# Low halves of W_in and of three more weight pieces: from VectorE and GpSimd to VectorE alone, in the first phase of a hybrid decoder layer

## The chip, the cores and the metric

The kernel runs on one core of one Trainium2 chip. The metric is device time in microseconds of one execution; lower is better. The time before is the median of three runs, 245.26 us (245.08 to 245.63).

## The reference, cut to what matters

One layer on a sequence of 512 rows and 1024 columns, float32 throughout:

```
shift, scale, gate = SiLU(c) @ W_ada + b_ada
h = RMSNorm(x) * (1 + scale) + shift
z = h @ W_in          # [lru_x | lru_gate | q | k | v | attn_gate], 3072 columns
lru_x -> causal conv(4) -> block-diagonal gates -> linear recurrence -> * SiLU(lru_gate)
q, k, v -> per-head RMS norm of q, k -> block attention (256-row blocks) -> * SiLU(attn_gate)
out = x + gate * (concat(groups) @ W_out)
```

Products must have nearly float32 precision. The kernel gets it by splitting each operand into a high half (rounded to the format that TensorE multiplies fast) and a low half, low = value - high, and by adding three products: high by high, low by high and high by low.

## The kernel before, in words

**Tiling.** The contraction runs over 1024 columns, so over eight slices (k = 0 to 7) of 128. Phase 1 computes the first 896 columns of `z`, transposed: four tiles xl0 to xl3 (the recurrent input) and three tiles gl0 to gl2 (its gate), seven PSUM banks that accumulate over the eight slices. For each slice, TensorE runs 14 matmuls with the high half of h (against the high and low weight) and then 7 with the low half of h (against the high weight): 21 matmuls of 512 columns, in a fixed order.

**What a slice needs.** From memory come a 1 MB piece of W_ada (`st`, in two halves) and a 0.45 MB piece of W_in in two parts, `wa` (512 columns) and `wb` (384). For slices 2 to 7, VectorE makes scale and shift from `st` with two dot products against the broadcast SiLU(c) (L442) and two tiny steps (`gs`, L483 and L484). ScalarE then writes h in float32 (`hf`, L495) and its high half (`h2h` and so on, L503), and VectorE the low half (`h2l`, L267). The weights are split by `split` (L271): the high half is a copy (`wA2h`, `wB2h`, L257, nearly all on ScalarE) and the low half a subtraction (`wA2l`, `wB2l`, L267).

**After phase 1.** VectorE and ScalarE read the seven banks: a convolution for each xl tile (`xc`, one ScalarE step L632 and three VectorE steps L635) and tanh-based SiLU for each gl tile (`gg`, L641 and L642). TensorE goes on with k: four row tiles k0 to k3, first half of the contraction with weight piece 0, second half with piece 1; then q with pieces 2 and 3, v with 8 and 9. k0 goes into bank 3, and k1, k2, k3 into banks 0, 1, 2, which gl0, gl1 and gl2 held: k1 can start when gg0 has been read out. A weight piece is 1 MB (`w_piece`, L554): one DMA into a staging buffer `wp0`, `wp1`, ..., four high halves and four low halves of 512 columns each (`w0_0h`, `w0_0l` to `w0_3l`). There are three staging buffers, shared by `st` and `wp` pieces: a piece's DMA is issued when the last reader of an older piece is done. In the profile numbers are left out of a name in places, so `w_2l` may be the third low half of any piece. Between the halves of k come `pr` (L654), the gates' block-diagonal products, which need xc.

**What sets the order.** A planner (`Plan`, L66 to L218) takes every step with its cost on each engine that may run it and a due time, and builds one list for each engine by a list schedule in estimated time. The lists are then fixed: each engine works through its own strictly in order, waiting on semaphores. Where a step may run on several engines, the planner takes the one that by its estimate finishes first. A subtraction of `split` may go to VectorE or GpSimd, unless `dve_only` is set; it was set for slices 0 and 1. The planner also knows a lock, so that in its estimate VectorE and GpSimd don't work at the same time where both use SBUF:

```
    def locks(o, e):
        return e == "POOL" or (e == "DVE" and o.sbuf)
```

Of the kernel before, what the change touches and what calls it, by code (L numbers as in the profile page):

```python
# [31 lines left out]
RESERVE = 10  # L32
SAME, SWITCH = 0.13, 0.1
EPS_PICK, ALPHA = 0.2, 0.1
NPE = 2
NSTAGE = 3
NC1 = 896
T0, TK, LEAD, NWARM, WSTEP, DIP = 14.5, 5.2, 4.0, 18, 0.35, 0.8
RAW, EPS0, ALPHA0, LATER = 3, 0.35, 1.0, 15.5
# [23 lines left out]
class Plan:  # L63
# [10 lines left out]
    def slot(self, name, dt=F32, n=512):  # L74
        return Buf(name, "slot", dt, n)
# [13 lines left out]
    def op(self, fn, costs, reads=(), writes=(), out_lat=None, dl=None, rel=0.0, window=None, sbuf=None, bulk=False, bias=None, mode="full"):  # L89
        o = Op(len(self.ops), fn, costs, out_lat)  # L90
        o.mode = mode
        o.bulk, o.bias = bulk, self.bias if bias is None else bias
        o.est, o.sbuf, o.free = rel, True, window
        for lst, wr in ((reads, False), (writes, True)):
            for x in lst:
                b, key = x if isinstance(x, tuple) else (x, None)
                if b.prev is not None:
                    o.preds.update(b.prev.ops)
                for k2, (ws, rs) in b.state.items():
                    if key is None or k2 is None or key == k2:  # L100
                        o.preds.update(ws)
                        if wr:
                            o.preds.update(rs)
                if wr:
                    if key is None:
                        b.state = {}
                    b.state[key] = ([o], [])
                else:
                    b.state.setdefault(key, ([], []))[1].append(o)
                if not b.ops or b.ops[-1] is not o:  # L110
                    b.ops.append(o)
                o.bufs.append(b)
                if b.kind == "bank":
                    o.sbuf = False
        if sbuf is not None:
            o.sbuf = sbuf
        o.preds.discard(o)
        for p in o.preds:
            p.succs.append(o)
        o.own = "PE" in costs and dl is None  # L120
        if "PE" in costs:
            o.dl = o.want = self.pe_t
            self.pe_t += costs["PE"]
        if dl is not None:
            o.dl = dl
        self.ops.append(o)
        return o
# [93 lines left out]
def c_act(n, ap=0, ps=False):  # L221
    return (0.052 if ps else 0.095) + n / 1200 + 0.093 * ap
# [15 lines left out]
def hybrid_layer_kernel(ctx: ExitStack, tc, x, small, call, bgate, wbd, wad, w1, wp, out):  # L238
# [8 lines left out]
    def fixed(name, shape, dt=F32):  # L247
        return Buf(name, "fixed", t=cp.tile(shape, dt, name=name))


    def copy(dst, d_ap, src, s_ap, n, psum=False, scale=None, reads=(), bulk=False, bias=None):

        ap = 0 if scale is None else 1

        def fn(e):
            if e is act:
                act.activation(d_ap(), s_ap(), AF.Copy, scale=1.0 if scale is None else scale())  # L257
            elif scale is None:
                dve.tensor_copy(d_ap(), s_ap())
            else:  # L260
                dve.tensor_scalar(d_ap(), s_ap(), scale(), None, op0=MULT)
        return op(fn, {"ACT": c_act(n, ap, psum), "DVE": c_dve(n, ap, psum, not psum)}, [src, *reads], [dst],
                  bulk=bulk, bias=bias)

    def tt(dst, d_ap, a, a_ap, b, b_ap, n, alu, psum=False, dve_only=False, rel=0.0):
        def fn(e):
            e.tensor_tensor(d_ap(), a_ap(), b_ap(), op=alu)  # L267
        costs = {"DVE": c_dve(n)} if psum or dve_only else c_tt(n)
        return op(fn, costs, [a, b], [dst], rel=rel)

    def split(src, s_ap, n, name, bulk=False, dve_only=False, rel=0.0):  # L271

        h, l = slot(name + "h", F32R, n), slot(name + "l", F32R, n)
        copy(h, lambda: h.t[:, :n], src, s_ap, n, bulk=bulk)
        tt(l, lambda: l.t[:, :n], src, s_ap, h, lambda: h.f()[:, :n], n, SUB,
           dve_only=dve_only, rel=rel)
        return h, l


    def dma(fn, mb, writes, extra=0.0, **kw):  # L280
        ndma[0] += 1
        if ndma[0] < 45 and "dl" not in kw:
            kw["dl"] = 0.001 * ndma[0]
        return op(lambda e: fn(), {"DMA": 0.05 + mb * 2.55 + extra}, [], writes, out_lat=2.0, **kw)
# [44 lines left out]
    def mk_gm(e):  # L329
# [4 lines left out]
                                 op1=MULT)  # L334
        dve.tensor_scalar(gm.t[:, NPE:, :], gm.t[:, NPE:, :], 0.5, None, op0=MULT)
    op(mk_gm, {"DVE": 0.6}, [sm], [gm, ga_], sbuf=False)
# [53 lines left out]
    for t in range(NT):  # L390
        w = xw[t // 2]
# [26 lines left out]
    NA, NB = 512, NC1 - 512  # L418
# [9 lines left out]
    hh, hl, ada, W1 = [None] * KT, [None] * KT, {}, {}  # L428

    def load_ada(k):  # L430
# [3 lines left out]
        for q in range(2):  # L434
            dma(lambda q=q: sp.dma_start(st.t[:, q * 1024:(q + 1) * 1024], wad[k, :, q * 1024:(q + 1) * 1024]), 0.5,
                [(st, q)], (DIP, 0.1, 0.1)[k] if k < 3 and q == 0 else 0.0)
        if k >= NPE:
            m = ada[k] = fixed(f"m{k}", [P, 2])
# [24 lines left out]
    def load_w(k):  # L463
        a, b = slot(f"wa{k}"), slot(f"wb{k}", n=NB)
        dma(lambda: sp.dma_start(a.t, w1[k, :, :512]), 0.25, [a])
        dma(lambda: sp.dma_start(b.t[:, :NB], w1[k, :, 512:]), 0.25 * NB / 512, [b])
        W1[k] = (split(a, lambda: a.t, 512, f"wA{k}", dve_only=k < 2, rel=0.0 if k else LATER),
                 split(b, lambda: b.t[:, :NB], NB, f"wB{k}", dve_only=k < 2, rel=0.0 if k else LATER))

    def gs_make(k):  # L470
        if k < NPE:
            acc = ada[k]

            def mm(e):
                for o in (0, 1):
                    pe.matmul(misc.t[:, 2 * k + o:2 * k + o + 1], acc.t[:, o * P:(o + 1) * P], ones.t[:, 0:1], start=True,
                              stop=True)
            op(mm, {"PE": 0.46}, [acc, ones], [(misc, k)], dl=T0 - 1.8 if k == 0 else T_[k] - 7.0)
        src = (misc, k) if k < NPE else ada[k]

        def mk(e):
            m, g = misc.t[:, 2 * k:2 * k + 2] if k < NPE else ada[k].t, gs.t[:, k, :]
            dve.tensor_tensor(g, m, gm.t[:, k, :], op=MULT)  # L483
            dve.tensor_tensor(g, g, ga_.t[:, k, :], op=ADD)  # L484
        op(mk, {"DVE": 0.3}, [src, gm, ga_], [(gs, k)], sbuf=False)
# [30 lines left out]

    load_ada(0)
    load_w(0)
    cb = fixed("cb", [P, D])
    load_ada(1)  # L520
    gs_make(0)
    h_make(0)
    load_w(1)
    for i in range(2):
        c_ = slot(f"c{i}")
        dma(lambda i=i, c_=c_: sp.dma_start(c_.t, call[:, i * 512:(i + 1) * 512]), 0.25, [c_])
        v = lambda i=i: cb.t[:, i * 512:(i + 1) * 512]
        op(lambda e, v=v, c_=c_: act.activation(v(), c_.t, AF.Tanh, scale=0.5), {"ACT": c_act(512, 0)}, [c_], [(cb, i)],
           dl=T_[NPE] - 8.0)
        op(lambda e, v=v, c_=c_: dve.scalar_tensor_tensor(v(), v(), 1.0, c_.t, op0=ADD, op1=MULT),  # L530
# [3 lines left out]
    gs_make(1)  # L534
    h_make(1)
    load_w(2)
    load_ada(3)
    for k in range(KT):
# [15 lines left out]
    def w_piece(i, n=4):  # L554
        st = Buf(f"wp{i}", "stage")
        dma(lambda: sp.dma_start(st.t[:, :n * 512], wp[i, :, :n * 512]), 0.25 * n, [st])
        return [split(st, lambda j=j: st.t[:, j * 512:(j + 1) * 512], 512, f"w{i}_{j}", True) for j in range(n)]

    def gated_w(dh, c, cn):

# [315 lines left out]
    zb = [3, 0, 1, 2]  # L876
    kb_ = [bank(f"k{t}", zb[t]) for t in range(4)]
    z_half(kb_, w_piece(0), True, True, [None, None, None, lambda: (gates(0, (4, 5)), gates(1, (6, 7)))])
    z_half(kb_, w_piece(1), True, False, [None, None, lambda: (gates(2, (4, 5)), gates(3, (6, 7)))])
    for t in range(4):  # L880
        qk_norm(kb_[t], ("k", t))
    qb_ = [bank(f"q{t}", zb[t]) for t in range(4)]
    z_half(qb_, w_piece(2), True, True, [None] + [lambda t=t: qk_tr(("k", t), 4 + t) for t in range(3)])
    lru_sqrt()
    z_half(qb_, w_piece(3), True, False, [lambda: qk_tr(("k", 3), 7)])
# [33 lines left out]
    for i in range(len(items)):  # L919
# [11 lines left out]
        a, hps = items[i]  # L931
# [17 lines left out]
    n = 0  # L949
    for o in pl.schedule():  # L950
        for b in o.bufs:
            if b.t is None:
# [5 lines left out]
                else:  # L958
                    w = b.n if b.kind == "slot" else 2048
# [64 lines left out]
```

## Time and profile before

| | |
|---|---|
| median of three runs | 245.26 us |
| the profiled execution, its own time | 243.45 us |
| its span, first to last instruction | 241.6 us |
| TensorE busy | 230.7 us, 95% |
| VectorE busy | 176.9 us, 73% |
| ScalarE busy | 140.4 us, 58% |
| GpSimd busy | 72.5 us, 30% |
| TensorE clock granted, mean | 0.999 |

All rows in the text come from the one profiled execution. PE is TensorE, DVE VectorE, ACT ScalarE, POOL GpSimd, and SP or SPq is SyncE, whose queue issues every DMA. A row of a timeline has the start in us from the span's beginning, the duration, engine, line of the kernel, operation, what is written and read with its shape, and in brackets the idle time ahead of it with the instruction that ended it. Consecutive instructions of one engine overlap by some tens of ns, so a cost is best read as the distance from one start to the next.

### The profile page before, as it was taken

To read this page: it belongs to the slowest core of one execution; us is meant where nothing else is said; L and a number is where in the kernel's file an instruction comes from. 1 tells how busy PE (TensorE), PEld (TensorE's weight loads), DVE (VectorE), ACT (ScalarE), POOL (GpSimd) and SP (SyncE) were. 2 spreads that over 40 slices of the span, in tenths; PEclk is the share of its full clock that TensorE was granted. 3 is DMA by queue.
4 is the path that set the end of the run, shared out by engine and by line. 5 is a ranking of instruction groups with operands and counts; after the bars stand their busy time and mean duration, and the time that the engine had idled before them with its cause. 6 is when DMAs were issued, how large, how long until landed. Compare 5 with 4: busy or idle time off the path is not lost.

```text
span 241.6 us, 3603 instructions
## 1 busy us (share of the span) xinstructions
PE 230.7 (95%) x1270; PEld 183.3 (76%) x1270; DVE 176.9 (73%) x389; ACT 140.4 (58%) x287; POOL 72.5 (30%) x66
## 2 busy tenths in 40 slices
PE   8899997999599999999999999999999999999994
PEld 8666875787387778888888768777777888788894
DVE  0779999979998578459667488596999996287221
ACT  5856453498528796334034379998999997131000
POOL 3300443207531462449320211329047122000001
PEclk9999999999999999999999999999999999999999
DMA  6999998770670402510470863000006012812221
GB/s 223 351 404 401 399 383 278 255 275 39 226 297 0 174 0 88 195 68 1 152 255 30 343 203 152 1 0 20 27 0 254 9 53 77 260 46 88 90 84 47
DMA packets 11879, 37.77 MB, mean 156 GB/s; under 512 B 1362, under 2 KB 3922, under 8 KB 9812
## 3 DMA queue, kind: packets, MB, share of 16 engines
q1 hardware_dynamic: 11860, 37.53, 42.7%
q8 instruction: 10, 0.16, 0.3%
q14 instruction: 9, 0.07, 0.1%
HBM read 35.43 MB, written 2.10 MB: 155 GB/s over the span
## 4 chain that ended last, share of the span: by engine, by line
PE 65%; DVE 18%; DMA 9%; ACT 5%; issue 2%; SPq 1%; DVEq 0%; ACTq 0%
PE u L842 19%; PE g L866 9%; PE q L616 9%; PE k L616 8%; PE v L616 6%; DVE st L442 5%; PE PT L803 4%; PE pv L820 4%; DMA st<-in_wad_dram 4%; DMA c<-in_call_dram 3%; PE S L765 3%; DVE ga L590 2%; DMA wg<-in_wp_dram 2%; PE pr L654 1%; DVE w_2l L267 1%
## 5 line engine op out<-in xcount | busy, mean ns | idle before, releaser
L778 ACT ACTIVATE P<-P,st 128x512 f32<-128x512 f32 (+3 forms) x32 | 17.6, 556 | 3.6 <-DVE st L775 3.6
L442 DVE SCALAR_TENSOR_TENSOR st<-st,cb 128x1024 f32<-128x1024 f32 x12 | 17.6, 1494 | 0.0
L787 POOL TENSOR_SCALAR P<-P,st 128x384 f32<-128x384 f32 (+3 forms) x13 | 9.0, 698 | 25.6 <-DVE st L781 25.6
L267 DVE TENSOR_TENSOR o<-u,gbc 128x512 f32<-128x512 f32 (+1 forms) x8 | 5.3, 658 | 14.5 <-PE u L842 14.5
L495 ACT ACTIVATE hf<-xs,gs 128x512 f32<-128x512 f32 x8 | 6.5, 814 | 15.8 <-DVE gs L484 15.8
L775 DVE CUSTOM_DVE_ANT_0 P<-S,maskf 128x512 f32<-128x512 f32 (+3 forms) x32 | 14.3, 481 | 0.9 <-PE g L866 0.9
L590 DVE SCALAR_TENSOR_TENSOR ga<-wg,cs,ga 128x512 f32<-128x512 f32 x16 | 12.8, 833 | 2.1 <-DMA wg<-in_wp_dram 2.1
L257 ACT ACTIVATE pt<-PT 128x384 f32<-128x384 f32 (+1 forms) x23 | 11.1, 526 | 3.4 <-PE PT L803 3.2
L267 POOL TENSOR_TENSOR w_1l<-wp,w_1h 128x512 fp32r<-128x512 f32 x4 | 6.4, 1599 | 20.5 <-ACT w_1h L257 13.8
L803 PE MATMUL PT<-ident,P 128*128 128x128 f32 x80 | 11.4, 277 | 0.3 <-ACT P L785 0.3
L803 PEld LDWEIGHTS PT<-ident,P 128*128 128x128 f32 x80 | 9.0, 141 | 3.1 <-issue 1.1
L267 POOL TENSOR_TENSOR o<-xr,o 128x256 f32<-128x256 f32 x1 | 0.7, 738 | 34.6 <-DVE o L267 34.6
L711 POOL TENSOR_TENSOR msk<-msk,nhalf 128x8 f32<-128x8 f32 x4 | 7.0, 1757 | 11.0 <-DVE msk L709 11.0
L820 PE MATMUL pv<-pt,vt 128*64 128x256 f32 (+1 forms) x96 | 10.0, 350 | 0.0
L711 POOL TENSOR_TENSOR msq<-msq,nhalf 128x8 f32<-128x8 f32 x4 | 7.8, 1952 | 6.0 <-DVE msq L709 5.9
L267 DVE TENSOR_TENSOR w_0l<-wp,w_0h 128x512 fp32r<-128x512 f32 x10 | 8.5, 849 | 1.5 <-ACT w_0h L257 1.5
L785 ACT ACTIVATE P<-P,st 128x128 f32<-128x128 f32 (+3 forms) x19 | 9.5, 544 | 0.0
L820 PEld LDWEIGHTS pv<-pt,vt 128*64 128x64 f32 x96 | 6.4, 136 | 4.0 <-issue 1.2
L257 ACT ACTIVATE qTh<-Tq 128x512 fp32r<-128x512 f32 x4 | 2.4, 598 | 11.2 <-PE Tq L723 11.2
L267 POOL TENSOR_TENSOR w_3l<-wp,w_3h 128x512 fp32r<-128x512 f32 x4 | 5.6, 1408 | 9.7 <-ACT w_3h L257 9.7
L635 DVE SCALAR_TENSOR_TENSOR xc<-xl,sm,xc 128x511 f32<-128x511 f32 (+2 forms) x12 | 8.0, 732 | 0.0
L422 PE MATMUL warm<-warm 128*128 128x128 bf16 x72 | 6.7, 277 | 1.0 <-DVE warm L304 1.0
(718 smaller groups left out, 787.6 us busy)
## 6 DMA issues: line engine op xcount, KB each, us to landing
wp<-in_wp_dram SPq DMA_DIRECT2D x12, 1024.0 KB, 4.8
st<-in_wad_dram SPq DMA_DIRECT2D x16, 512.0 KB, 7.5
wg<-in_wp_dram SPq DMA_DIRECT2D x4, 1024.0 KB, 4.8
x<-in_x_dram SPq DMA_DIRECT2D x4, 512.0 KB, 5.5
wa<-in_w_dram SPq DMA_DIRECT2D x8, 256.0 KB, 7.7
xr<-in_x_dram SPq DMA_DIRECT2D x7, 256.0 KB, 2.8
out_dram<-o SPq DMA_DIRECT2D x7, 256.0 KB, 2.0
wb<-in_w_dram SPq DMA_DIRECT2D x8, 192.0 KB, 7.5
```

What stands on the lines that cost most here:

```text
L257: act.activation(d_ap(), s_ap(), AF.Copy, scale=1.0 if scale is None else scale())
L267: e.tensor_tensor(d_ap(), a_ap(), b_ap(), op=alu)
L442: dve.scalar_tensor_tensor(v, v, 1.0, cb.t, op0=MULT, op1=MULT, accum_out=m.t[:, q:q + 1])
L590: dve.scalar_tensor_tensor(gacc[hf].t, w, cs.t[:, d:d + 1], gacc[hf].t, op0=MULT, op1=ADD)
L616: pe.matmul(acc.t, hx[kt].t[:, a * P:(a + 1) * P], wx.t, start=s0, stop=s1)
L711: op(lambda e: pool.tensor_tensor(m.t, m.t, nhalf.t, op=ALU.pow), {"POOL": 1.65}, [nhalf], [m])
L775: op(lambda e: dve.tensor_tensor_reduce(p_.t[:, :n], b.t[:, c0:c0 + n], maskf.t[:, 512 - n:], -1.0, -NEG, op0=ADD, op1=ALU.min, accum_out= ...
L778: op(lambda e: act.activation(p_.t[:, :n], p_.t[:, :n], AF.Exp, bias=st.t[:, 0:1], scale=-1.0, accum_out=st.t[:, 1:2]), {"ACT": c_act(n, 2 ...
L803: pe.transpose(b.t[:, o_:o_ + P], p_.t[:, kb * P:(kb + 1) * P], ident.t)
L820: pe.matmul(b.t[64 * e_:64 * e_ + 64, h0 + o_:h0 + o_ + n], vt[kb].t[:, hd * 64:(hd + 1) * 64], pt[e_, kb // 2].t[:, 256 * (kb % 2):256 * ...
L842: pe.matmul(b.t[:, :cn], y_.t[:, c0:c0 + P], w.t[:, cw:cw + cn], start=kt == 0 and i == 0, stop=kt == KT - 1 and i == 2)
L866: pe.matmul(b.t, wx.t[:, c0:c0 + P], hx[kt].t, start=kt == 0 and p == 0, stop=kt == KT - 1 and p == 2)
```

## The change

A constant `NDV = 3` is added, and `dve_only` is set in three calls of `split`: for both parts of W_in in all eight slices (before: slices 0 and 1), and for the weight pieces 0, 1 and 2. Their subtractions may then run on VectorE only. Nothing else is written differently.

```
+NDV = 3
...
-        W1[k] = (split(a, lambda: a.t, 512, f"wA{k}", dve_only=k < 2, rel=0.0 if k else LATER),
-                 split(b, lambda: b.t[:, :NB], NB, f"wB{k}", dve_only=k < 2, rel=0.0 if k else LATER))
+        W1[k] = (split(a, lambda: a.t, 512, f"wA{k}", dve_only=True, rel=0.0 if k else LATER),
+                 split(b, lambda: b.t[:, :NB], NB, f"wB{k}", dve_only=True, rel=0.0 if k else LATER))
...
-        return [split(st, lambda j=j: st.t[:, j * 512:(j + 1) * 512], 512, f"w{i}_{j}", True) for j in range(n)]
+        return [split(st, lambda j=j: st.t[:, j * 512:(j + 1) * 512], 512, f"w{i}_{j}", True, dve_only=i < NDV) for j in range(n)]
```

The planner then builds other lists. TensorE's list is the same, row for row. GpSimd's loses eleven subtractions and gains one. Its list between the last step for x and the gates, before (the added line makes every line number one larger afterwards):

```order
L267 TENSOR_TENSOR wA2l_59_463<-wa2_47_412,wA2h_53_445 128x512
L267 TENSOR_TENSOR wA3l_69_513<-wa3_54_447,wA3h_63_487 128x512
L267 TENSOR_TENSOR wA4l_81_570<-wa4_65_494,wA4h_74_540 128x512
L267 TENSOR_TENSOR wA5l_92_622<-wa5_73_535,wA5h_78_560 128x512
L267 TENSOR_TENSOR wA6l_103_671<-wa6_82_577,wA6h_88_606 128x512
L267 TENSOR_TENSOR wA7l_115_720<-wa7_90_616,wA7h_98_646 128x512
L267 TENSOR_TENSOR w1_3l_138_801<-wp1_102_665,w1_3h_123_749 128x512
L267 TENSOR_TENSOR w2_0l_142_817<-wp2_113_714,w2_0h_127_765 128x512
L267 TENSOR_TENSOR w2_1l_146_830<-wp2_113_714,w2_1h_129_771 128x512
L267 TENSOR_TENSOR w2_2l_149_843<-wp2_113_714,w2_2h_132_780 128x512
L267 TENSOR_TENSOR w2_3l_150_852<-wp2_113_714,w2_3h_148_836 128x512
L267 TENSOR_TENSOR xcs0l_153_865<-xc0_134_786,xcs0h_151_855 128x512
```

All but the last are gone from GpSimd's list afterwards; it goes from the steps for x straight to xcs0l, and does w8_2l much later, which VectorE did before. The second place is VectorE's list in phase 1, from the end of slice 2's dots on (`gs` is scale and shift, `po` a chain of twelve small steps for the softplus of the recurrence, which ends in `sp4` and `sn4`). Before:

```order
L483 TENSOR_TENSOR gs_93<-m2_95,gm_74 128x2
L484 TENSOR_TENSOR gs_93<-gs_93,gad_75 128x2
L358 TENSOR_SCALAR po_82<-z2_81 128x4
L360 SCALAR_TENSOR_TENSOR po_82<-po_82,z2_81 128x4 x3
L267 TENSOR_TENSOR wB2l_61_480<-wb2_49_419,wB2h_55_451 128x384
L442 SCALAR_TENSOR_TENSOR st3_50_425,m3_96<-st3_50_425,cb_94 128x1024 x2
L267 TENSOR_TENSOR h2l_68_509<-hf2_60_470,h2h_62_482 128x512
L483 TENSOR_TENSOR gs_93<-m3_96,gm_74 128x2
L484 TENSOR_TENSOR gs_93<-gs_93,gad_75 128x2
L360 SCALAR_TENSOR_TENSOR po_82<-po_82,z2_81 128x4 x4
L267 TENSOR_TENSOR wB3l_71_530<-wb3_57_457,wB3h_64_491 128x384
```

VectorE at the same place now:

```order
L484 TENSOR_TENSOR gs_93<-m2_95,gm_74 128x2
L485 TENSOR_TENSOR gs_93<-gs_93,gad_75 128x2
L268 TENSOR_TENSOR wA2l_59_467<-wa2_47_412,wA2h_53_445 128x512
L268 TENSOR_TENSOR wB2l_61_473<-wb2_49_419,wB2h_55_451 128x384
L443 SCALAR_TENSOR_TENSOR st3_50_425,m3_96<-st3_50_425,cb_94 128x1024 x2
L268 TENSOR_TENSOR h2l_68_503<-hf2_60_469,h2h_62_478 128x512
L484 TENSOR_TENSOR gs_93<-m3_96,gm_74 128x2
L485 TENSOR_TENSOR gs_93<-gs_93,gad_75 128x2
L268 TENSOR_TENSOR wA3l_69_511<-wa3_54_447,wA3h_63_483 128x512
L268 TENSOR_TENSOR wB3l_71_520<-wb3_57_457,wB3h_64_487 128x384
```

In each of the slices 2 to 7 a wA subtraction has come in, and the softplus steps are gone: they now stand behind weight piece 3, among the first steps of k's norm. The third place is VectorE's list at the end of phase 1, ahead of the first xc and gg steps. Before:

```order
L267 TENSOR_TENSOR w1_0l_131_777<-wp1_102_665,w1_0h_114_716 128x512
L267 TENSOR_TENSOR w1_1l_133_784<-wp1_102_665,w1_1h_116_724 128x512
L267 TENSOR_TENSOR w1_2l_135_790<-wp1_102_665,w1_2h_121_742 128x512
L635 SCALAR_TENSOR_TENSOR xc0_134_786<-xl0_32_366,sm_63,xc0_134_786 128x511
L642 SCALAR_TENSOR_TENSOR gg0_136_794<-gg0_136_794,gl0_39_381 128x512
```

The same stretch of VectorE's list now:

```order
L268 TENSOR_TENSOR w1_0l_129_751<-wp1_101_647,w1_0h_113_696 128x512
L268 TENSOR_TENSOR w1_1l_130_757<-wp1_101_647,w1_1h_121_724 128x512
L268 TENSOR_TENSOR w1_2l_132_763<-wp1_101_647,w1_2h_123_730 128x512
L268 TENSOR_TENSOR w1_3l_134_769<-wp1_101_647,w1_3h_125_736 128x512
L268 TENSOR_TENSOR w2_0l_136_776<-wp2_112_692,w2_0h_131_761 128x512
L268 TENSOR_TENSOR w2_1l_138_783<-wp2_112_692,w2_1h_133_767 128x512
L636 SCALAR_TENSOR_TENSOR xc0_137_780<-xl0_32_366,sm_63,xc0_137_780 128x511
L643 SCALAR_TENSOR_TENSOR gg0_139_788<-gg0_139_788,gl0_39_381 128x512
```

w1_3l, w2_0l and w2_1l have come in ahead of xc0 and gg0; w2_2l and w2_3l follow behind the last xc step. On ScalarE, the cast w1_0h moves ahead of hf7, and the cast w3_3h changes engines with w3_0h (ScalarE and VectorE). On SyncE, the DMA of wp1 moves ahead of that of `wbd`, the gates' weights.

## The prediction

> **What bounds the kernel now.** I read the page first: TensorE is busy for 95% of the span, so the question is where its few gaps lie. The view of who TensorE waited for names them (engine and line that waited, whom for; total us, times, longest).
>
> ```profile
> PE k L616 <- DVE gg L642: 2.9, 1, 2.9
> PE xl L514 <- DVE h3l L267: 1.2, 1, 1.2
> ```
>
> Both end on VectorE. Next comes TensorE's timeline through phase 1 (start, duration, what it computes).
>
> ```profile
> 27.99 0.39 PE L514 MATMUL xl<-h2h,wA2h 128*128 128x512 f32 x1
> ...
> 49.93 0.40 PE L514 MATMUL xl<-h6h,wA6h 128*128 128x512 f32 x1
> ...
> 54.72 0.50 PE L514 MATMUL xl<-h7h,wA7h 128*128 128x512 f32 x1
> ...
> 58.05 1.07 PE L514 MATMUL xl<-h7l,wA7h 128*128 128x512 f32 x4
> ...
> 59.63 0.39 PE L616 MATMUL k<-w_0h,h0h 128*128 128x512 f32 x1
> ...
> 62.13 0.39 PE L616 MATMUL k<-w_3l,h3h 128*128 128x512 f32 x1
> 65.38 0.50 PE L616 MATMUL k<-w_0h,h0h 128*128 128x512 f32 x1 [2.86 <-DVE gg L642]
> ...
> 73.76 0.50 PE L654 MATMUL pr<-xcs0h,wbdh 64*128 64x512 f32 x2
> ```
>
> The six slices 2 to 7 take 59.63 - 27.99 = 31.64 us. The slice that never waited is slice 6: 54.72 - 49.93 = 4.79. Six of those are 28.74, so phase 1 loses 2.90 us after slice 2 starts. The twelve matmuls of k0 take 62.13 - 59.63 + 0.23 (the usual step, 4.79/21) = 2.73; k1 could start at 62.36 and starts at 65.38, 3.02 later. Together 5.92 us of TensorE gaps, which VectorE causes. Its own timeline shows how.
>
> ```profile
> 24.10 1.78 DVE L267 TENSOR_TENSOR h1l<-hf,h1h 128x512 fp32r<-128x512 f32 x1
> ...
> 26.06 0.16 DVE L358 TENSOR_SCALAR po<-z 128x4 f32<-128x4 f32 x1
> 26.26 0.56 DVE L360 SCALAR_TENSOR_TENSOR po<-po,z 128x4 f32<-128x4 f32 x3
> 26.73 0.56 DVE L267 TENSOR_TENSOR wB2l<-wb,wB2h 128x384 fp32r<-128x384 f32 x1
> 27.21 1.22 DVE L442 SCALAR_TENSOR_TENSOR st<-st,cb 128x1024 f32<-128x1024 f32 x1
> ...
> 28.35 2.31 DVE L442 SCALAR_TENSOR_TENSOR st<-st,cb 128x1024 f32<-128x1024 f32 x1
> ...
> 30.59 0.68 DVE L267 TENSOR_TENSOR h2l<-hf,h2h 128x512 fp32r<-128x512 f32 x1
> 31.20 0.15 DVE L483 TENSOR_TENSOR gs<-m,gm 128x2 f32<-128x2 f32 x1
> ...
> 31.46 0.75 DVE L360 SCALAR_TENSOR_TENSOR po<-po,z 128x4 f32<-128x4 f32 x4
> ...
> 54.76 0.69 DVE L267 TENSOR_TENSOR h7l<-hf,h7h 128x512 fp32r<-128x512 f32 x1 [1.92 <-issue]
> ...
> 55.97 1.79 DVE L267 TENSOR_TENSOR w_2l<-wp,w_2h 128x512 fp32r<-128x512 f32 x1
> ...
> 61.09 1.78 DVE L267 TENSOR_TENSOR w_0l<-wp,w_0h 128x512 fp32r<-128x512 f32 x1
> 62.79 0.68 DVE L267 TENSOR_TENSOR w_1l<-wp,w_1h 128x512 fp32r<-128x512 f32 x1
> 63.39 0.68 DVE L267 TENSOR_TENSOR w_2l<-wp,w_2h 128x512 fp32r<-128x512 f32 x1
> 63.99 0.74 DVE L635 SCALAR_TENSOR_TENSOR xc<-xl,sm,xc 128x511 f32<-128x511 f32 x1
> 64.65 1.87 DVE L642 SCALAR_TENSOR_TENSOR gg<-gg,gl 128x512 f32<-128x512 f32 x3
> 66.44 7.30 DVE L635 SCALAR_TENSOR_TENSOR xc<-xl,sm,xc 128x511 f32<-128x511 f32 x11
> ```
>
> The same 512-wide subtraction takes 0.68 us in one row and 1.78 in another, and a dot 1.22 or 2.31. What stands beside the long rows is on GpSimd's timeline; these are five of its eleven rows between 23 and 66 us, the first and last among them.
>
> ```profile
> 23.91 1.42 POOL L267 TENSOR_TENSOR wA2l<-wa,wA2h 128x512 fp32r<-128x512 f32 x1 [12.77 <-ACT wA2h L257]
> 28.26 1.32 POOL L267 TENSOR_TENSOR wA3l<-wa,wA3h 128x512 fp32r<-128x512 f32 x1 [2.94 <-ACT wA3h L257]
> ...
> 55.79 1.42 POOL L267 TENSOR_TENSOR w_3l<-wp,w_3h 128x512 fp32r<-128x512 f32 x1 [8.47 <-ACT w_3h L257]
> 57.17 1.73 POOL L267 TENSOR_TENSOR w_0l<-wp,w_0h 128x512 fp32r<-128x512 f32 x1
> ...
> 63.55 1.65 POOL L267 TENSOR_TENSOR w_3l<-wp,w_3h 128x512 fp32r<-128x512 f32 x1 [1.24 <-ACT w_3h L257]
> ```
>
> h1l (24.10) begins inside wA2l, the long dot (28.35) inside wA3l, w_2l (55.97) inside w_3l. Ten of the eleven GpSimd rows have one long VectorE row beside them, each about 1.1 us too long. The eleventh (63.55) runs beside xc, which reads its first operand from PSUM, and xc keeps 0.74.
>
> The Trainium skill, "SBUF — State Buffer", section "Who interferes with whom", says that a VectorE instruction with two SBUF inputs is blocked by a GpSimd instruction that reads SBUF, for the whole instruction. The trace agrees in which rows suffer; it shows 1.1 us a time, not the whole 1.3 to 1.4.
>
> **The change part by part.** *Removed:* ten stalls. A subtraction alone steps in 62.79 to 63.39 = 0.60; stalled it is 1.78 - 0.68 = 1.10 longer, the dot 2.31 - 1.22 = 1.09. Ten make 11.0 us of VectorE. *Added ahead of xc:* nine subtractions (wA2l to wA7l, w1_3l, w2_0l, w2_1l) at 0.60 = 5.4; w2_2l and w2_3l come behind the xc rows. The price lies between 0.60 and the stalled 1.70; I take 0.60, since no GpSimd row is left beside them. *Moved out:* the twelve small softplus rows (po, then sp4 and sn4), four of which take 26.73 - 26.06 = 0.67, so 2.0; their result goes to the gates' exponentials, far behind. *Idle:* 1.92 before h7l can go too.
>
> So VectorE could reach xc at 63.99 - 11.0 + 5.4 - 2.0 - 1.9 = 54.5. The slices say the same: wA 0.60, wB 27.21 - 26.73 = 0.48, two dots at 1.14 (28.35 - 27.21), the h subtraction 0.61 (31.20 - 30.59) and gs 0.26 (31.46 - 31.20) make 4.23 a slice. That is below TensorE's 4.79. VectorE is no longer the bound in phase 1, and TensorE's path becomes it: 27.99 + 28.74 = 56.73 for k0, plus 2.73 = 59.46 for k1. Gain there: 65.38 - 59.46 = 5.92.
>
> What is late next? ScalarE and the transfers, in these rows.
>
> ```profile
> 56.00 0.64 ACT L257 ACTIVATE w_0h<-wp 128x512 fp32r<-128x512 f32 x1 [0.28 <-DMA wp<-in_wp_dram]
> 58.48 0.78 ACT L632 ACTIVATE xc<-xl,sm 128x512 f32<-128x512 f32 x1 [0.80 <-PE xl L514]
> 59.38 1.58 ACT L641 ACTIVATE gg<-gl 128x512 f32<-128x512 f32 x3
> ```
>
> ScalarE's xc starts 0.43 after the row at 58.05, when xl0 is complete; 2.9 earlier that is 55.6, done 56.4. VectorE's xc then waits for it from 54.5, and gg0 runs about 57.1 to 57.8, before k1 needs its bank at 59.46: 1.7 to spare. Later work keeps the lead: the fifteen xc and gg rows took 63.99 to 73.74, so they end near 56.4 + 9.8 = 66.2, and pr, which needs them, moves to 73.76 - 5.9 = 67.9.
>
> Three moves follow. On ScalarE the cast w1_0h now stands ahead of hf7, so slice 7's h waits for wp1: issued when st6's dots are done, near 41.0, landed near 45.8 by the time below, h7h ready near 47.6, wanted at 56.73 - 4.79 = 51.9. On SyncE wp1 goes ahead of wbd, which is wanted only for pr. And GpSimd now does w8_2l, which can stall VectorE by 0 to 1.1 us (I take 1.1), while the softplus rows (2.0) land among the k-norm rows. What hides both is VectorE's idle there: it is busy for 7.18 of the 12 us from 78 to 90 (first row below), and without that cover they would cost up to 3.1.
>
> The transfers must keep up. The rows are two stretches of the engines' busy times (TensorE, weight loads, VectorE, ScalarE, GpSimd, then clock, DMA share, GB/s), and the time from issue to landing of the weight pieces issued between 40 and 60 us.
>
> ```profile
> 78.00:90.00 12.00, 12.00 (x59) 9.41 (x58) 7.18 (x13) 10.61 (x17) 6.60 (x4) 1.00 0.24 87
> ```
>
> ```profile
> 0.00:36.00 36.00, 32.85 (x222) 25.54 (x223) 27.11 (x72) 21.71 (x42) 9.60 (x17) 1.00 0.97 360
> DMA to landing us min/median/max: 4.7/4.7/4.8
> ```
>
> By the sizes in the code, st7 is complete after 14.3 MB; at 360 GB/s that is 39.7 us. VectorE wants it at 24.96 (h1l's 24.10 + 0.60 + 0.26) + 4 x 4.23 + 1.08 = 43.0. wp2 is issued when those dots are done, 45.3, and lands at 50.0; its two casts and two subtractions fit before 54.5.
>
> Nothing after k1 changes on TensorE, whose order is the same row for row. Span 241.6 - 5.9 = 235.7; the profiled execution's 243.45 becomes 237.5. That execution lies 1.81 below the median of 245.26, so the median forecast is **239.4 us**.
>
> **The rivals.** *A, half given back.* w2_0l and w2_1l now stand on VectorE ahead of xc, so wp2's landing can hold gg0, and everything on VectorE behind it. For: before, these were GpSimd's, and VectorE's order is strict. Against: it costs only if wp2 lands after 56.3 (59.46 less two xc/gg rows of 0.66, two subtractions and a cast of about 0.6 each), 11 us after its issue, where the row says 4.8. If it decided so far that the k1 gap stayed, only phase 1's 2.9 is won: 242.4; if phase 1 kept its waits and only that gap closed, 3.0: 242.3.
>
> *B, slower.* The long rows are long for another reason than GpSimd, and VectorE simply gets more work. Then xc moves by 5.4 - 2.0 = 3.4 later, or 1.5 if the 1.92 of idle absorbs its part, and k1 with it: 246.8 to 248.7, say 247.7. It decides if less than 1.5 of the 11.0 us vanish. For: VectorE is full from 24 to 65 us, GpSimd mostly idle. Against: ten coincidences out of ten, and the PSUM reader unhurt.
>
> The Trainium skill speaks for B in "Perfetto Trace Analysis", section "Optimizing Scalar/DVE Operations": with a saturated VectorE, moving work even to GpSimd may make sense, and this change does the reverse. The same paragraph adds that the two share a port, so that such a move might not help.
>
> *C, no change.* Some wait behind k1 that I take for slack absorbs all 5.9. The nearest I see is pr, with 67.9 against 66.2; it would have to slip by 7.6.
>
> **How the numbers follow.** The forecast has 0.68: gains of 5.4 to 6.4, so 238.9 to 239.9, for the spread of slices (4.79, up to 0.1 more where TensorE restarts). A has 0.22, spread from 239.9 to 242.4. B 0.05, C 0.02, and 0.03 for more than the forecast's best. The range takes the forecast, the 0.03 and the smaller half of A: 238.7 to 241.5. A measurement of this kernel can tell about 0.2%, 0.5 us, from no change. Faster: 0.68 + 0.22 + 0.03 = 0.93; same 0.02; slower 0.05.
>
> **What would show it.** Right: no row of 1.7 us or a 2.3 us dot on VectorE before xc; six slices of about 4.8 on TensorE; no wait for gg before k1, which starts near 59.5; VectorE waiting for ScalarE before xc. Wrong: long rows without GpSimd beside them (B), xc on VectorE starting after 58.1 with wp2's cast waiting for DMA (A), or a new TensorE wait behind 60 us (C).

## The result, and the profile after

The changed kernel takes 237.12 us (median of six executions, 236.95 to 237.47). The kernel before takes 245.19 in the six beside it (244.97 to 245.63). The ratio is 0.967, interval 0.9658 to 0.9683: faster by 8.07 us, where 5.9 was forecast. The profiled execution of the changed kernel is an ordinary one: 237.1 us, span 235.3.

TensorE's list of waits, after (what it waited for; total us, times, longest), holds no wait for gg or h3l any more. Its longest wait is now at the start, for x.

```profile
PE xT L379 <- DMA x<-in_x_dram: 1.3, 1, 1.3
...
PE PT L804 <- ACT P L786: 0.3, 1, 0.3
...
PE xl L515 <- DVE h0h L498: 0.2, 1, 0.2
```

TensorE's timeline, after, at the places that were shown of before:

```profile
27.93 0.39 PE L515 MATMUL xl<-h2h,wA2h 128*128 128x512 f32 x1
...
51.73 0.39 PE L515 MATMUL xl<-h7h,wA7h 128*128 128x512 f32 x1
...
56.49 0.39 PE L617 MATMUL k<-w_0h,h0h 128*128 128x512 f32 x1
...
59.21 0.39 PE L617 MATMUL k<-w_0h,h0h 128*128 128x512 f32 x1
...
67.47 0.50 PE L655 MATMUL pr<-xcs0h,wbdh 64*128 64x512 f32 x2
```

Slices 2 to 7 take 56.49 - 27.93 = 28.56 us instead of 31.64, and k1 follows k0 without a gap. It starts 65.38 - 59.21 = 6.17 earlier; the span is 241.6 - 235.3 = 6.3 shorter. GpSimd, which had eleven subtractions between 23 and 66 us, now idles there until its first step for the gates; the number in brackets is its idle time.

```profile
62.19 1.29 POOL L268 TENSOR_TENSOR xcs0l<-xc,xcs0h 128x512 fp32r<-128x512 f32 x1 [50.62 <-ACT xcs0h L258]
```

VectorE's timeline, after:

```profile
24.03 0.69 DVE L268 TENSOR_TENSOR h1l<-hf,h1h 128x512 fp32r<-128x512 f32 x1
...
49.12 0.69 DVE L268 TENSOR_TENSOR h7l<-hf,h7h 128x512 fp32r<-128x512 f32 x1 [1.29 <-ACT h7h L504]
...
55.14 0.69 DVE L268 TENSOR_TENSOR w_1l<-wp,w_1h 128x512 fp32r<-128x512 f32 x1
56.15 0.75 DVE L636 SCALAR_TENSOR_TENSOR xc<-xl,sm,xc 128x511 f32<-128x511 f32 x1 [0.32 <-ACT xc L633]
56.87 1.88 DVE L643 SCALAR_TENSOR_TENSOR gg<-gg,gl 128x512 f32<-128x512 f32 x3
58.67 7.30 DVE L636 SCALAR_TENSOR_TENSOR xc<-xl,sm,xc 128x511 f32<-128x511 f32 x11
```

No long row is left ahead of the xc rows: h1l takes 0.69 instead of 1.78. The page of the profile shows the same for all twelve dots of the slices 2 to 7 (mean 1219 ns; the long ones of before took 2.31 us):

```profile
L443 DVE SCALAR_TENSOR_TENSOR st<-st,cb 128x1024 f32<-128x1024 f32 x12 | 14.3, 1219 | 0.0
```

So the profile shows 6.3 us, about what was forecast for it (5.9). The medians differ by 1.8 more. The profiled execution of before took 243.45, 1.7 to 1.8 less than its median; that of the changed kernel lies on its median. The experiments had to find this 1.8 first.

### The profile page after: what moved, and what is told of

The parts are those of the page before. It is cut to its first block, busy times and chain, and to the rows that moved or that the text cites. A ratio compares the mean times of both kernels' runs of the same rounds, so it can differ in the third digit from the quotient of the medians.

```text
span 235.3 us, 3590 instructions
## 1 busy us (share of the span) xinstructions
PE 228.5 (97%) x1270; PEld 183.9 (78%) x1270; DVE 173.0 (74%) x399; ACT 140.7 (60%) x287; POOL 55.4 (24%) x56
## 4 chain that ended last, share of the span: by engine, by line
PE 83%; DMA 9%; DVE 3%; ACT 2%; SPq 1%; issue 0%; DVEq 0%
PE u L843 19%; PE k L617 9%; PE g L867 9%; PE q L617 9%; PE xl L515 9%; PE gl L515 7%; PE v L617 6%; PE PT L804 4%; PE pv L821 4%; DMA st<-in_wad_dram 4%; DMA c<-in_call_dram 3%; PE S L766 3%; DVE ga L591 2%; DMA wg<-in_wp_dram 2%; PE pr L655 1%; ACT P L779 1%
## 5 line engine op out<-in xcount | busy, mean ns | idle before, releaser
L443 DVE SCALAR_TENSOR_TENSOR st<-st,cb 128x1024 f32<-128x1024 f32 x12 | 14.3, 1219 | 0.0
L268 POOL TENSOR_TENSOR xcs0l<-xc,xcs0h 128x512 fp32r<-128x512 f32 x1 | 1.3, 1294 | 50.6 <-ACT xcs0h L258 50.6
L268 POOL TENSOR_TENSOR w_1l<-wp,w_1h 128x512 fp32r<-128x512 f32 x3 | 4.6, 1537 | 20.5 <-ACT w_1h L258 13.8
```

What stands on the lines that cost most here:

```text
L443: dve.scalar_tensor_tensor(v, v, 1.0, cb.t, op0=MULT, op1=MULT, accum_out=m.t[:, q:q + 1])
```

## The experiments

Letters in the expectations: L, the stalls that GpSimd's subtractions cause on VectorE are the gain; Q, the order and balance of VectorE's list is the gain; P, ordinary executions of before have more stalled VectorE rows than the profiled one; S, the 1.8 us lie elsewhere than in phase 1. The clock theory came out of the first profile below; the granted clock is the share of its full speed at which TensorE's clock ran. Each experiment was timed beside runs of before on the same chip, whose median was 244.9 to 245.0 in every series.

**The kernel before, twice more,** with no edit, to get a profile of an ordinary execution.

> The kernel before, unchanged, for a second trace. Its runs have a median of 245.19 us, but the profiled one took 243.45, and the forecast carried that 1.7 to 1.8 us over to the changed kernel, whose profiled run and median agree (237.1). Theory P: which of VectorE and GpSimd gets to SBUF first varies from execution to execution; an ordinary one has one or two more stalled VectorE rows of 1.1 us between 24 and 65 us than the profiled one. Then this profile, if it is an ordinary one (span 243.2 to 243.8), has TensorE's k1 start at 66.8 to 67.5 instead of 65.38, and everything behind k1 as long as before (176.2 us). Rival S: the 1.8 us lie outside that stretch, in the start-up or behind k1; then k1 starts at 65.4 again while the span is 243.4. If the span is 241.6 again, this trace decides nothing.

> The same kernel before once more, since one trace may fall on either side. As for the second trace: theory P expects a span of 243.2 to 243.8 to come with k1 at 66.8 to 67.5, rival S with k1 at 65.4; a span of 241.6 comes with k1 at 65.4 by both.

Measured: 245.46 us with span 243.7 and mean granted clock 0.992; and 243.31 with span 241.5 and clock 0.999. The first is the ordinary kind. Of its 2.1 us of longer span, 0.3 lie ahead of slice 2; the rest lies behind the wait. TensorE's timeline there, from the wait before k1 on:

```profile
65.68 0.73 PE L616 MATMUL k<-w_0h,h0h 128*128 128x512 f32 x1 [2.87 <-DVE gg L642]
66.21 0.63 PE L616 MATMUL k<-w_0h,h0l 128*128 128x512 f32 x1
...
68.77 0.59 PE L616 MATMUL k<-w_2h,h2l 128*128 128x512 f32 x1
69.19 0.40 PE L616 MATMUL k<-w_2l,h2h 128*128 128x512 f32 x1
...
70.14 0.39 PE L616 MATMUL k<-w_0h,h0h 128*128 128x512 f32 x1
```

The wait is as long as in the first profile (2.86), but the matmuls behind it step by 0.43 us instead of 0.23 until 69.19. k1 takes 70.14 - 65.68 = 4.46, against 2.73 for k0: 1.73 us lost. The view of busy times by stretch names the reason: behind the stretch and its length stand TensorE's busy time, those of weight loads, VectorE, ScalarE and GpSimd, and then the granted clock. The first row is this execution, the second the profile shown of before.

```profile
66.00:68.00 2.00, 2.00 (x6) 1.52 (x6) 2.00 (x4) 0.00 (x0) 0.00 (x0) 0.50 0.77 328
```

```profile
66.00:68.00 2.00, 2.00 (x10) 1.64 (x9) 2.00 (x4) 0.00 (x0) 0.00 (x0) 1.00 1.00 422
```

The clock is 0.50 here and 1.00 there; TensorE gets 6 matmuls done instead of 10. P falls (the same ten rows are long, k1 starts at 65.68, not 66.8), and S holds, at this place. The clock stays at 0.50 from about 65.8 to 69.2 us, 3.4 us, which costs half of that and lowers the mean over the span by 1.7 / 243.7 = 0.007. So the mean clock tells the kinds of before apart: of the 55 executions of before timed beside these runs, 17 have 0.999 or 1.0 and take 243.2 to 243.8 us, 33 have 0.991 to 0.993 and 244.7 to 245.5, five have 0.986 and 246.1 to 246.5. The profile that the prediction was made from is of the rarer first kind.

**Either half of the change alone.** W_in only:

```
-NDV = 3
+NDV = 0
```

> One half of the change: W_in's low parts on VectorE only, the weight pieces free to go to either engine (NDV = 0). GpSimd then does w0_0l, w2_2l and w2_3l in this stretch, three rows instead of eleven. Theory L (a GpSimd subtraction beside a VectorE instruction with two SBUF inputs holds that up by 1.1 us, and these stalls are all of the gain): phase 1 on TensorE has six slices of 4.8, VectorE is up to 2.2 us later at xc than in the changed kernel, which eats its slack of about 2 there; k1 starts at 59.2 to 60.0, time 237.0 to 238.0 us. Rival Q (the gain comes from the other order and balance of the lists, the softplus rows out of phase 1 above all, and not from stalls): the softplus steps are out of the slices here too, so 237.1 as well, but then the three GpSimd rows have no long VectorE row beside them.

Measured: 237.37 (237.30 to 237.61), ratio 0.9722 [0.9682, 0.9763]; k1 follows k0 without a gap, at 59.24. W_in's part alone gains all but about 0.25. Weight pieces only (edit against the changed kernel):

```
-    W1[k] = (split(a, lambda: a.t, 512, f"wA{k}", dve_only=True, rel=0.0 if k else LATER),
-             split(b, lambda: b.t[:, :NB], NB, f"wB{k}", dve_only=True, rel=0.0 if k else LATER))
+    W1[k] = (split(a, lambda: a.t, 512, f"wA{k}", dve_only=k < 2, rel=0.0 if k else LATER),
+             split(b, lambda: b.t[:, :NB], NB, f"wB{k}", dve_only=k < 2, rel=0.0 if k else LATER))
```

> The other half: the low parts of weight pieces 0 to 2 on VectorE only, W_in as before (GpSimd does wA2l to wA7l). Theory L: the six stalls of phase 1 stay, and so do TensorE's 2.9 us in the slices; the four stalls of 1.1 behind them are gone, VectorE reaches xc 4.4 us earlier less nothing, and the 3.0 us in front of k1 go: 240.4 us by the profiled run of before, and 242.2 if the 1.8 us by which ordinary runs are longer lie in the slices. Rival Q: the softplus rows stay where they were and the lists of phase 1 are those of before, so nothing is gained there and little behind: 243 to 245.

Measured: 240.30 (240.20 to 240.81), ratio 0.9848 [0.9797, 0.9898]; the clock is 0.998 or more in all four. Six long rows stay in phase 1, but TensorE no longer waits before k1:

```profile
59.48 0.39 PE L617 MATMUL k<-w_0h,h0h 128*128 128x512 f32 x1
...
62.20 0.39 PE L617 MATMUL k<-w_0h,h0h 128*128 128x512 f32 x1
```

k1 starts 3.2 us earlier than in before (65.38), yet the time is 4.6 below the median of before beside it (244.92): the fall of the clock goes with the gap. VectorE's softplus rows stand here where they stood in before (from 25.95 on), so this gain owes nothing to their move. The halves gain 7.6 and 4.6 and together 7.8: they don't add up, since either one closes the gap before k1.

With W_in alone, GpSimd keeps three subtractions in this stretch. One (at 45.40) holds a VectorE row up by 1.1 us (`gs` at 45.82 takes 1.25 instead of 0.15). GpSimd's timeline shows the other two:

```profile
53.01 4.18 POOL L268 TENSOR_TENSOR w_2l<-wp,w_2h 128x512 fp32r<-128x512 f32 x1 [5.96 <-DVE w_0l L268]
...
60.45 1.30 POOL L268 TENSOR_TENSOR w_3l<-wp,w_3h 128x512 fp32r<-128x512 f32 x1 [3.26 <-ACT w_3h L258]
```

The first takes 4.18 us instead of 1.30, beside five VectorE subtractions of 0.69 each that follow one another without a gap: here GpSimd was the one held up.

**The clock theory, tested from both sides.** First the wait of before is filled with products of a tile of zeros (`zw`, made by one small VectorE row at the start), all else in its place:

```
...
+            for _ in range(12):
+                pe.matmul(kb_[0].t, zw.t, hh[0].t, start=False, stop=False)
...
```

> The kernel before, with twelve matmuls of zero weights (adding 0 to k0) put after the first half of k0, to keep TensorE busy while it waits for VectorE; nothing else is moved. Twelve times 0.2275 = 2.73 us, less than the wait of 2.87 before k1, so k1 can start where it did (65.3 to 65.7). Clock theory (the wait itself makes the granted clock fall to 0.50 for some 3.4 us, which costs 1.7): no execution shows it, all come at 243.2 to 243.7 with a clock of 0.998 or more, about 1.7 below the ordinary execution of before on this chip (244.9). Rival (the clock falls for another reason, or the 1.7 us lie elsewhere): both kinds of execution as in before, 243.4 and 245.0, median 245.

Measured: 243.44 (243.12 to 243.85), the clock 0.998 or more in all twelve executions; ratio 0.995 [0.9927, 0.9974] against before, whose 23 executions beside it were of all kinds: seven with the clock at 0.999 or 1.0 (243.45 to 243.65) and 16 below.

```profile
62.18 2.96 PE L883 MATMUL k<-h0h,zw 128*128 128x512 f32 x12
...
65.19 0.50 PE L618 MATMUL k<-w_0h,h0h 128*128 128x512 f32 x1
```

k1 starts about where it did in the first profile (65.19 against 65.38; k0 too starts 0.18 earlier), and the median falls by 1.5 us through useless work in the wait. Then the wait is put into the changed kernel, with seven, six and five idle VectorE rows ahead of gg0:

```
+        if name == "gg0":
+            op(lambda e: [dve.tensor_tensor(maskf.t, maskf.t, maskf.t, op=MAX) for _ in range(7)],
+               {"DVE": 0.001}, [], [g, maskf])
```

> The changed kernel with seven idle subtraction-sized rows (the mask's maximum with itself, 128x512) put on VectorE ahead of gg0, so that TensorE waits before k1 again though GpSimd does nothing in phase 1. Seven rows of 0.60 to 0.69 are 4.2 to 4.8 us; gg0 has about 1.6 to spare (it ends at 57.6, k1 starts at 59.2), so the wait is 2.6 to 3.2 us. Clock theory: two kinds of execution, 240.0 (237.1 + 2.9) without and 241.7 with a clock that falls to 0.50 after the wait, the second the more frequent, with a mean clock of about 0.992. Rival (the clock's fall belongs to GpSimd's work or to something else in before): one kind, 239.7 to 240.3, clock 0.998.

> As the run with seven idle rows ahead of gg0, with six. Seven made TensorE wait 3.13 us before k1; one row is worth 5.04 / 7 = 0.72, so the wait is 2.41 us and the time without a fall of the clock 237.1 + 2.4 = 239.5. Clock theory, gradual form (a wait that is shorter than some window of fixed length only sometimes fills it): fewer executions with the fall than the twelve of twelve at 3.13 us and the sixteen to nineteen of thirty at 2.87: some at 241.2 with a clock of 0.992, more at 239.5 with 0.998 or over. Rival form (any wait of over 2 us drops the clock): all at 241.2.

> As above with five rows: a wait of 3.13 - 2 x 0.72 = 1.69 us, 238.8 without a fall. Clock theory, gradual form: no or hardly any execution with the fall (clock 0.998 or over in all), 238.6 to 239.0. Rival form (any wait drops the clock by as much): 240.4 to 240.6.

The wait of TensorE with seven, six and five rows, each from the list of waits:

```profile
PE k L617 <- DVE gg L646: 3.1, 1, 3.1
```

```profile
PE k L617 <- DVE gg L646: 2.4, 1, 2.4
```

```profile
PE k L617 <- DVE gg L646: 1.7, 1, 1.7
```

| wait before k1 | time | executions with a lower clock |
|---|---|---|
| 3.13 us (seven rows) | 242.42 (241.66 to 244.23) | 12 of 12 (five of them at 0.986, 243.2 to 244.2) |
| 2.87 us (before) | see above | 38 of 55 |
| 2.41 us (six rows) | 239.56 to 240.05 without, 241.1 and 241.5 with | 2 of 6 |
| 1.68 us (five rows) | 239.11 (238.68 to 239.31) | 0 of 6 (0.997 or more) |

The clock falls without any work of GpSimd beside it, and the longer the wait, the more often; the counts at 2.41 and 1.68 us are small. The gradual form of the theory fits; "any wait over 2 us" falls. Where none of these waits exists, the fall is rare: of 42 executions of the changed kernel and the other variants without a wait before k1, two have a lower mean clock (0.992 and 0.991, both in the tries on the softplus below; not profiled). A lower mean alone does not prove lost time: in the changed kernel's profile the clock is 0.83 in the last 3.3 us, when TensorE has nothing left to do. With seven rows the fall does not come at once: the clock by stretch is

```profile
62.00:64.00 2.00, 1.50 (x7) 1.25 (x8) 2.00 (x4) 0.00 (x0) 0.00 (x0) 1.00 0.04 8
64.00:66.00 2.00, 2.00 (x6) 1.61 (x5) 2.00 (x4) 0.00 (x0) 0.00 (x0) 0.50 0.00 0
```

so k1 starts at 62.50 at full clock and is slowed from 64.0 on, again for 3.4 us. With six rows, in the one of the two executions with the fall that was profiled, it is slowed almost from its start (61.84).

**Is it GpSimd's reading that stalls VectorE?** Eleven idle rows on GpSimd in the changed kernel, at the places of its old subtractions, VectorE's list untouched (`EXTRA` names wA2 to wA7, w1_3 and w2_0 to w2_3; `idle` tells the planner that these rows lock nothing, so that it leaves the lists as they are). First products, which read SBUF:

```
+        if name in EXTRA:
+            op(lambda e: pool.tensor_tensor(maskf.t[:, :384], maskf.t[:, :384], h.f()[:, :384], op=MULT), {"POOL": 0.001}, [h], [maskf]).idle = True
```

> The changed kernel, VectorE's list untouched, with eleven extra products on GpSimd in phase 1 (the mask's zero columns times a high part, 128x384, about 1.0 us each), at the times when GpSimd did the eleven subtractions. Lock theory (a GpSimd row that reads SBUF holds up a VectorE row with two SBUF inputs): long VectorE rows (over 1.3 us, or a dot over 1.8) return, about 0.8 us each, up to eleven of them; VectorE has about 3 us to spare on the way to gg0, so the time is 238.3 to 243.5, middle 241, with waits of TensorE in phase 1 or before k1. Order theory (the gain is from the order of VectorE's list, not from stalls): 237.1 and no long rows. Third possibility, from the run with W_in's low parts alone on VectorE: GpSimd is the one that is held out, its rows grow long, VectorE's don't: 237.1 to 238.

Measured: 238.68 (238.55 to 238.95). GpSimd's and VectorE's timelines:

```profile
23.70 1.14 POOL L279 TENSOR_TENSOR maskf<-maskf,wA2h 128x384 f32<-128x384 f32 x1 [12.32 <-ACT wA2h L258]
...
54.64 5.42 POOL L279 TENSOR_TENSOR maskf<-maskf,w_3h 128x384 f32<-128x384 f32 x1 [8.79 <-ACT w_3h L258]
60.14 1.02 POOL L279 TENSOR_TENSOR maskf<-maskf,w_0h 128x384 f32<-128x384 f32 x1
```

```profile
23.89 1.50 DVE L268 TENSOR_TENSOR h1l<-hf,h1h 128x512 fp32r<-128x512 f32 x1
...
55.50 0.69 DVE L268 TENSOR_TENSOR w_0l<-wp,w_0h 128x512 fp32r<-128x512 f32 x1
```

h1l and the four next low parts of h are 0.81 longer (1.50 against 0.69), and end 0.55 after GpSimd's row does (25.39 against 24.84): GpSimd first, then VectorE. A sixth row, `gs` at 35.41, takes 0.97 instead of 0.15. At the end of phase 1 it is the other way round again: one GpSimd row takes 5.42, the VectorE rows beside it none longer than 0.69. Six stalls, 5 x 0.81 + 0.82 = 4.87 us of VectorE, cost 1.6 us of time. Then memsets, which only write:

```
-            op(lambda e: pool.tensor_tensor(...), {"POOL": 0.001}, [h], [maskf]).idle = True
+            op(lambda e: pool.memset(maskf.t[:, :384], 0.0), {"POOL": 0.001}, [h], [maskf]).idle = True
```

> The same eleven places, but GpSimd only writes (a memset of the mask's zero columns, 128x384), and reads nothing from SBUF. Lock theory: no long VectorE rows, 237.0 to 237.3. If any work of GpSimd holds VectorE up: as in the run with the products, 238.3 to 243.5.

Measured: 237.07 (236.91 to 237.38). This decides nothing: having nothing to read, the memsets waited for nothing and ran before phase 1's slices, as GpSimd's timeline shows.

```profile
10.92 5.43 POOL L279 MEMSET maskf<- 128x384 f32 x11
```

So each was held back by a product of one column, `pool.tensor_tensor(maskf.t[:, :1], maskf.t[:, :1], h.f()[:, :1], op=MULT)`:

> The run with GpSimd only writing, once more, because there the eleven memsets had nothing to wait for and all ran at 10.9 to 16.4 us, ahead of the stretch in question. Now each is held back by a product of one column with the same high part (128x1, too short to matter), so that it runs where GpSimd's subtractions stood. Lock theory (only a GpSimd row that reads SBUF holds VectorE up): no VectorE row lengthened by over 0.2 us, 237.0 to 237.4. If any row of GpSimd does it: five or more rows of h's low halves at about 1.1 instead of 0.69 (a memset takes 0.4 to 0.5), as with the products 238 to 239.

Measured: 237.09 (237.02 to 237.39). GpSimd and VectorE:

```profile
24.24 0.42 POOL L280 MEMSET maskf<- 128x384 f32 x1
27.34 1.09 POOL L279 TENSOR_TENSOR maskf<-maskf,wA3h 128x1 f32<-128x1 f32 x1 [2.67 <-ACT wA3h L258]
```

```profile
24.06 0.69 DVE L268 TENSOR_TENSOR h1l<-hf,h1h 128x512 fp32r<-128x512 f32 x1
...
27.16 1.22 DVE L448 SCALAR_TENSOR_TENSOR st<-st,cb 128x1024 f32<-128x1024 f32 x1
```

The memset at 24.24 lies inside h1l, which keeps its 0.69. The one-column read at 27.34 needs 1.09 us, until the dot of 27.16 is over. L holds for reading; writing alone disturbs nothing.

**The softplus rows** that the planner moved out of phase 1. Three tries to put them back, by due times of 1, 30 and 26 us (in the last the planner was also given next to no cost for them):

```
-        op(lambda e: fn(), {"DVE": 0.13 * n}, reads, writes, sbuf=False, rel=rel)
+        op(lambda e: fn(), {"DVE": 0.13 * n}, reads, writes, sbuf=False, rel=rel, dl=1.0)
```

> The changed kernel with the softplus's small rows done early again, before the first slices, so that VectorE's gap at 70 to 76 us is not used and phase 1 gets their 2.0 us back. Theory: VectorE has slack in phase 1 now (it idles 1.29 us before h7l and 0.32 before xc0, and gg0 has 1.6 us to spare), no long rows: 237.0 to 237.6. Order theory (moving the softplus out was a part of the gain): 2.0 us later, 239.1.

> The changed kernel with the softplus's small rows put back into slices 2 and 3, where the kernel before had them (in the run that forced them early they stood ahead of the first slice and cost 0.7 us there); TensorE's list is the same. Slack theory: h2l is done at 28.96 and wanted at 27.93 + 14 x 0.2267 = 31.1, so VectorE has 2.1 us in hand and then gains 4.76 - 4.24 = 0.5 a slice; 2.0 us of small rows fit: 237.0 to 237.4. Order theory (moving the softplus out was a part of the gain of 8): 238 to 239.1.

> The softplus's rows in phase 1 once more, since in the run before it more than they had moved: h3l had gone to GpSimd (1.31 us, beside a VectorE row of 1.16 instead of 0.17) and on ScalarE hf6 behind two casts that waited for a transfer. Here the small rows stand between slice 2's and slice 3's steps (around 26 to 30 us), GpSimd does nothing in phase 1, and ScalarE's list differs there only in the place of three casts. Slack theory: 2.0 us fit into VectorE's lead; gs of slice 4, done at 33.46 in the changed kernel, comes at 35.3 to 35.5, its h high 1.5 later at 37.0, wanted at 37.44: 237.0 to 237.5. Order theory: the softplus itself was worth the 2.0 that the run before lost: 238.5 to 239.1.

Measured: 238.27 (238.16 to 238.43), 239.10 (238.08 to 239.17) and 237.78 (237.17 to 239.01). None is a clean answer. The first put them ahead of slice 0 and reordered TensorE's first transposes, so k0 starts at 57.17, 0.68 late; one of its executions has a clock of 0.992 and is no longer than the others (238.32). In the second the planner also gave h3l to GpSimd, beside which a VectorE row of 0.17 takes 1.16, and put ScalarE's hf6 behind two casts:

```profile
31.15 1.31 POOL L268 TENSOR_TENSOR h3l<-hf,h3h 128x512 fp32r<-128x512 f32 x1 [19.35 <-ACT h3h L504]
```

```profile
31.33 1.16 DVE L365 TENSOR_SCALAR sn<-sp 128x4 f32<-128x4 f32 x1
```

The third comes nearest. All twelve rows lie on VectorE between 24.8 and 30.5 us, GpSimd does nothing there, and the slices run at 4.76 us up to slice 6, softplus or not. VectorE is behind with the dots by then, so wp1 is issued at 42.57 instead of 41.09, and its cast on ScalarE, which waits for it, holds up hf7 and with it h7h:

```profile
49.84 0.63 ACT L258 ACTIVATE w_0h<-wp 128x512 fp32r<-128x512 f32 x1 [2.30 <-DMA wp<-in_wp_dram]
```

k0 starts 0.30 late (56.79), and the profiled execution took 237.44, 0.3 more than the changed kernel. The four executions spread over 1.8 us, one with a clock of 0.991 at the long end; the rest of the spread is not explained. So the profiles put the move of the softplus at some tenths and not at 2.0; the times give no closer figure.

**All low parts on VectorE,** for the later weight pieces too:

```
-NDV = 3
+NDV = 99
```

> The low parts of all sixteen weight pieces on VectorE, not of the first three only, so that GpSimd's 1.28 to 1.55 us subtractions are gone from phase 2 as well (eight or more of them, each of which can hold a VectorE row for 1.1 us). TensorE is busy 97% of the span now, and waits for neither VectorE nor GpSimd after 56 us by more than 0.3 us: there is nothing left to win for it, 236.8 to 237.4. Rival (VectorE becomes the bound in phase 2, since it is given about 8 x 0.60 = 4.8 us more there): 238 to 240.

Measured: 237.83 (237.67 to 237.89), 0.7 slower than the changed kernel. k0 starts at 56.56 (56.49 in the changed kernel); later TensorE waits for VectorE once more, in its list of waits:

```profile
PE g L867 <- DVE g L643: 0.3, 1, 0.3
```

The measured time lies between the two expectations: nothing more to win, and a small price. No kernel that ran is faster than the changed one by more than the scatter.

## Why the prediction was right and wrong

**The gaps of TensorE (5.92 forecast): right.** They shrank by 6.17 up to k1. Forecast were 2.90 in phase 1 (measured 31.64 - 28.56 = 3.08) and 3.02 before k1 (all of it).

**Ten stalls, 11.0 us: right in the cause.** All are gone, stalls come back when GpSimd reads and not when it only writes, and with the weight pieces alone the four behind the slices went, and the gap before k1 with them. The prediction read the 1.1 us as less than the whole GpSimd row. But the VectorE row begins after GpSimd's, and a subtraction ends 0.55 after it (in before h1l at 25.88, wA2l at 25.33), just as beside the idle products: it waits for what is left of GpSimd's row. The Trainium skill, "SBUF — State Buffer", section "Who interferes with whom", says that such a VectorE row contends with a GpSimd row that reads, not with one that only writes; the runs agree (0.81 longer, and not at all). But which engine is held up differs: in before VectorE and GpSimd took turns at the end of phase 1, in two experiments GpSimd stood by for 4.18 and 5.42 us. What decides this was not found.

**What is late next: right, with one row off.** ScalarE's xc starts at 55.34 (55.6 forecast), VectorE's gg0 at 56.87 (57.1), the xc rows end at 65.97 (66.2), pr starts at 67.47 (67.9). VectorE was forecast to be free for xc at 54.5 and is at 55.83, because it waits 1.29 us for h7h; the forecast had let all of the idle time there vanish. These rows of ScalarE show why:

```profile
47.08 0.63 ACT L258 ACTIVATE w_0h<-wp 128x512 fp32r<-128x512 f32 x1 [0.38 <-DMA wp<-in_wp_dram]
47.62 0.80 ACT L496 ACTIVATE hf<-xs,gs 128x512 f32<-128x512 f32 x1
48.45 0.63 ACT L504 ACTIVATE h7h<-hf 128x512 fp32r<-128x512 f32 x1
...
55.34 0.78 ACT L633 ACTIVATE xc<-xl,sm 128x512 f32<-128x512 f32 x1 [2.57 <-PE xl L515]
```

The cast of wp1 that now stands ahead of hf7 waited for its transfer, until 47.1 instead of the 45.8 forecast: it was issued at 41.1, as forecast, but took 6.0 us to land and not 4.8. h7h was ready at 49.08, wanted at 51.73: as forecast it cost TensorE nothing.

**The profiled execution, 237.5: right.** It took 237.1.

**The median: here the prediction failed.** The step was "That execution lies 1.81 below the median of 245.26, so the median forecast is 239.4". It took the distance between one execution and the median for a constant that a change leaves alone. It was a cost with a place: in most executions of before the wait of 2.87 us in front of k1 is followed by 3.4 us at half clock, which costs half of that, 1.7. The change removed this wait, and the 1.7 with it: 6.3 + 1.7 to 1.8 = 8.0 to 8.1. The term of the gap before k1 was 3.0 in the sum and is 3.0 + 1.7 = 4.7 in the median; the weight pieces alone, which close just this gap, measured 4.6. The clock was in the view by stretches, which the prediction read only for an execution without the fall; nothing in that trace shows it.

A rule of the Trainium skill would have pointed to this place: "TensorE: Matmul & The Clock Gate", section "HAM oscillation", says that TensorE should have no idle gaps of more than about 3.4 us, or its clock is halved again. By that figure 2.87 us would have been harmless; here it was not in 38 of 55 executions, and 2.41 not in two of six. The same page of the Trainium skill, Part 1, "What's actually happening", adds a window of that length that runs on without regard to the kernel. That fits that the fall comes in some executions only and up to 1.5 us after TensorE has started again; no run here shows the window itself.

**The rivals.** A (half given back) did not happen, since wp2's rows never held xc. B (slower, the long rows not due to GpSimd) is refuted by the time, and by the idle products. C needed a new wait behind k1, and there is none. For more gain than the forecast's best the prediction had 0.03, and no mechanism; the distance of 1.81 between profile and median, unexplained, was the sign that one was missing.

## What to carry to other kernels

Where the profiled execution lies off the median by more than the scatter, compare the granted clocks of the executions and ask which wait the difference hangs on, before carrying it over. A TensorE wait of two to three microseconds in the middle of dense work can cost its length and, as here, some 1.7 us more, so closing one can pay more than the trace shows, and filling one with useless matmuls can pay as well. Subtractions on GpSimd that read SBUF are not free beside VectorE rows with two SBUF inputs, even where GpSimd is idle most of the time.

## What the runs showed of the hardware that was not expected

The clock falls to 0.50 for about 3.4 us after many waits of 2.4 to 3.1 us, at once or up to 1.5 us after TensorE starts again, and did not after 1.7 (six executions). Executions with a mean clock of 0.986 instead of 0.992 are another 1.2 us or so longer, as if the fall came twice; none of them was profiled. A GpSimd read of a single column needs 1.09 us when it meets a VectorE dot. And a 128x4 VectorE row with one input in SBUF (`sn`, 0.17 us) took 1.16 beside a GpSimd subtraction. The changed kernel has another such row in phase 2 (`msk`, L710, 128x8, at 78.90: 1.29 instead of 0.17 beside GpSimd's subtraction at 78.88), so small rows with one input are not safe either.
